# Two heads' half-array products pinned side by side, the first branch's keys and values formed once, negated scores, and one step moved from VectorE to ScalarE

## The chip, the cores and the metric

One core of one Trainium2 chip runs the whole program as a single launch. The metric is the device time of one execution in microseconds (us).

## The reference, cut to what matters

Two transformer blocks of 512 tokens by 1024 features, run one after the other, all in fp32. The first block has two attention branches with 8 heads of 64 features each. The first branch selects keys with an indexer and attends to a 128-wide latent `c_kv`; the second is a stick-breaking attention.

```python
# first branch (dsa)
q_abs = einsum("bshd,hcd->bshc", q, w_uk)
rel   = relu(einsum("bqhe,bse->bqhs", q_idx, k_idx))          # indexer, 8 heads of 64
score = einsum("bqhs,bqh->bqs", rel, w_idx)                   # causal, then top_k(score, 128)
logits = einsum("bqhc,bqkc->bhqk", q_abs, c_sel) * 0.125 + rel_bias[bucket(distance)]
o = einsum("bqhc,hcd->bqhd", einsum("bhqk,bqkc->bqhc", softmax(logits), c_sel), w_uv)
# second branch (stick breaking)
z = einsum("bqhd,bshd->bhqs", q, k) * 0.125
a = exp(log_sigmoid(z) + reversed_exclusive_cumsum(log_sigmoid(-z)))   # strictly causal
o = einsum("bhqs,bshd->bqhd", a, v)
# second block, its first layer: latent attention, 8 heads, 64 + 32 rotary features
o = einsum("bhqk,bkhd->bqhd", softmax(mask(einsum("bqhd,bkhd->bhqk", q, k) * 96**-0.5)), v)
```

Around this lie the input projections, gates, output products, a mixture of 32 experts, a recurrence, a retention layer and two MLPs, which the change doesn't touch.

## The kernel before, in words

Everything is fp32. A projection of weights is three passes of split operands (high by high, high by low, low by high; `mm3`, lines 128 to 130), the attention products are plain fp32 and appear in the trace as two records each. Lines 106 and 107 split a tile into its high and low part (ScalarE, then VectorE).

The program is unrolled and hands its instructions to a scheduler that fixes each engine's order ahead of time: earlier program text goes first, later work fills in where the scheduler expects an engine to be free and a buffer is to be had. Projections of later stages are what fills TensorE in the attention loops. An engine works through its own queue in order. Tiles of one tag share a fixed number of buffers; the first stage has 19 of tag "z" (projected queries, keys, values, masks and gates) and eight PSUM banks, two each of tags "a" (projections), "l" (scores), "x" (transposes) and "o" (value sums).

The pieces that the change and the prediction touch, by line of the kernel before:

- The indexer (lines 234 to 256): for each of the query blocks i = 1, 2, 3 and each pair of heads, two score products with 64 rows each (line 242), one head on rows 0 to 63 of the array and the other on rows 64 to 127, each into a bank of its own, for W = (i+1) x 128 keys. ScalarE applies relu (245), VectorE adds up (249) and then finds the top 128 in 16 rounds (253, 254).
- The second branch (lines 300 to 327), for each head pair `hp` and query block `i`: two score products (306), the mask as a bf16 product (308), tanh on ScalarE (310), a memset and a scaling step on VectorE (311, 312), the scan (313) and a product (315), transposes on TensorE (318), a copy out of PSUM on ScalarE (320), and the value products (326), which put one head on columns 0 to 63 and the other on 64 to 127 of one bank; then a split (109, 110).
- The first branch (lines 332 to 382), for each half of the heads `hg` and query block: the query goes through `w_uk` (343) and out of PSUM (344); each head's scores are a product of all 128 rows with the latent (349), get the bias (352, 354), the selection mask and maximum (357), a sign flip of the maximum (361), exp (363) and the division (364, 365), then transposes (368), a copy (370) and the product with the latent (372). Four heads later one copy (374) and the product with `w_uv` (379), then the split.
- The latent attention in the second block (`softmax`, lines 1121 to 1135, and `attend`, lines 1137 to 1162): maximum, sign flip (1129), exp (1131), transposes (1152), copy (1154), value products by column halves (1160). Its stage has three banks "l", one "x" and one "o". Its scores have 96 rows (1147).

In all these loops the two products of a pair are two separate entries for the scheduler, and it may put other work between them.

## Time and profile before

| | us |
|---|---|
| median of 3 runs | 2307.77 (2306.92 to 2308.5) |
| profiled execution | 2308.01 |
| its span in the trace | 2305.8 |
| TensorE busy | 2215.8 |
| VectorE busy | 1241.2 |
| ScalarE busy | 895.7 |

The profile is one execution. Busy is the time in which at least one instruction of an engine runs; a product on TensorE counts until its last result is out, so successive products overlap by the tail, and how long one holds the queue is read from where the next one starts. The granted clock (PEclk) is TensorE's, as a share of 2.4 GHz. A view of waits lists who sat idle until whom. In the timeline, successive instructions of one line and engine are merged into a row: start, duration, engine, line, output and inputs, rows by columns of the array and columns streamed, and the number of records.

### The profile page before, as it was taken

How to read it: one execution, taken by the hardware profiler on the slowest of the kernel's cores; microseconds unless marked ns; L12 is line 12 of the kernel's file. 1: busy time of each engine (PE TensorE's matmuls, PEld its weight loads, DVE VectorE, ACT ScalarE, POOL GpSimd, SP SyncE). 2: the span in 40 equal slices, each digit the busy share in tenths (PEclk: the TensorE clock that was granted, in tenths of full speed). 3: DMA queues.
4: the chain of work that ended last, by engine and by line, in shares of the span. 5: the costliest groups of instructions: out<-in, count | busy, mean ns of one | idle time of the engine just before them, and what ended most of it. 6: DMA issues, size and time to landing. Idle time of an engine off the chain costs nothing.

```text
span 2305.8 us, 35750 instructions
## 1 busy us (share of the span) xinstructions
PE 2215.8 (96%) x14228; PEld 1836.5 (80%) x14228; DVE 1241.2 (54%) x2423; ACT 895.7 (39%) x1710; POOL 194.6 (8%) x247
## 2 busy tenths in 40 slices
PE   7999999969999999998999999999999998999998
PEld 5766778954444697778999999888888888989888
DVE  5976554633333677667544435745454547343436
ACT  5234542422122565665422324532323235332334
POOL 0000000111111001005000001501010104000000
PEclk9989999979999999999999999999999999999999
DMA  6211113759999541014323334232222122233233
GB/s 215 74 56 37 46 46 96 247 210 390 396 399 401 194 143 57 24 42 151 99 87 91 91 92 128 89 97 78 84 69 92 66 82 93 82 101 92 86 103 122
DMA packets 107465, 296.71 MB, mean 129 GB/s; under 512 B 17286, under 2 KB 19345, under 8 KB 107297
## 3 DMA queue, kind: packets, MB, share of 16 engines
q1 hardware_dynamic: 102656, 285.81, 36.9%
q0 software_dynamic: 3488, 6.50, 0.8%
q8 instruction: 113, 1.85, 0.3%
q10 hardware_dynamic: 1152, 2.10, 0.2%
q14 instruction: 56, 0.45, 0.1%
HBM read 292.31 MB, written 6.37 MB: 130 GB/s over the span
## 4 chain that ended last, share of the span: by engine, by line
PE 68%; DVE 4%; POOL 2%; ACT 2%; issue 1%; DMA 1%; POOLq 0%; DVEq 0%; ACTq 0%; SPq 0%
PE ps L128 18%; PE ps L129 17%; PE ps L130 17%; PE ps L725 5%; PE ps L762 3%; PE ps L749 2%; DVE wl L107 1%; POOL t L919 1%; PE ps L1147 1%; PE ps L1160 1%; PE ps L713 1%; DVE X L107 1%; ACT wh L106 1%; DVE N L882 0%; PE ps L1152 0%
## 5 line engine op out<-in xcount | busy, mean ns | idle before, releaser
L128 PE MATMUL ps<-X,wh 128*128 128x512 f32 (+3 forms) x1728 | 571.1, 332 | 16.8 <-ACT wh L106 10.4
L106 ACT ACTIVATE wh<-wr 128x1024 fp32r<-128x1024 f32 (+1 forms) x325 | 336.2, 1038 | 622.8 <-PE ps L129 431.3
L129 PE MATMUL ps<-X,wh 128*128 128x512 f32 (+3 forms) x1728 | 569.8, 330 | 3.8 <-DVE X L107 3.5
L130 PE MATMUL ps<-X,wl 128*128 128x512 f32 (+3 forms) x1728 | 568.1, 330 | 0.2 <-DVE wl L107 0.2
L107 DVE TENSOR_TENSOR wl<-wr,wh 128x1024 fp32r<-128x1024 f32 (+1 forms) x325 | 394.0, 1214 | 237.2 <-ACT wh L106 235.4
L128 PEld LDWEIGHTS ps<-X,wh 128*128 128x128 f32 x1728 | 325.7, 189 | 49.8 <-ACT wh L106 10.4
L129 PEld LDWEIGHTS ps<-X,wh 128*128 128x128 f32 x1728 | 326.9, 189 | 35.7 <-DVE X L107 7.0
L130 PEld LDWEIGHTS ps<-X,wl 128*128 128x128 f32 x1728 | 326.0, 189 | 31.3 <-issue 2.7
L130 PE MATMUL ps<-h,wl 128*128 128x256 f32 (+1 forms) x512 | 146.7, 287 | 0.7 <-DVE wl L107 0.7
L128 PE MATMUL ps<-h,wh 128*128 128x256 f32 (+1 forms) x512 | 146.3, 286 | 0.7 <-ACT wh L106 0.7
L129 PE MATMUL ps<-h,wh 128*128 128x256 f32 (+1 forms) x512 | 146.7, 287 | 0.0
L129 PE MATMUL ps<-wl,h 128*128 128x256 f32 x512 | 144.4, 282 | 0.7 <-DVE wl L107 0.7
L128 PE MATMUL ps<-wh,h 128*128 128x256 f32 x512 | 144.0, 282 | 0.4 <-ACT R L1471 0.3
L130 PE MATMUL ps<-wh,h 128*128 128x256 f32 x512 | 143.5, 281 | 0.0
L129 PE MATMUL ps<-wl,X 128*128 128x256 f32 x448 | 127.5, 285 | 0.5 <-DVE wl L107 0.5
L128 PE MATMUL ps<-wh,X 128*128 128x256 f32 x448 | 128.0, 286 | 0.0
L130 PE MATMUL ps<-wh,X 128*128 128x256 f32 x448 | 127.1, 284 | 0.0
L130 PEld LDWEIGHTS ps<-h,wl 128*128 128x128 f32 x512 | 97.3, 190 | 0.9 <-DVE wl L107 0.9
L128 PEld LDWEIGHTS ps<-h,wh 128*128 128x128 f32 x512 | 97.0, 190 | 1.1 <-ACT wh L106 1.1
L128 PEld LDWEIGHTS ps<-wh,h 128*128 128x128 f32 x512 | 96.6, 189 | 0.9 <-ACT R L1471 0.6
L129 PEld LDWEIGHTS ps<-h,wh 128*128 128x128 f32 x512 | 97.0, 189 | 0.0
L129 PEld LDWEIGHTS ps<-wl,h 128*128 128x128 f32 x512 | 96.1, 188 | 1.0 <-DVE wl L107 0.9
(467 smaller groups left out, 3846.4 us busy)
## 6 DMA issues: line engine op xcount, KB each, us to landing
wr<-in_mlp_w_dram SPq DMA_DIRECT2D x104, 512.0 KB
X<-in_w_gu_dram SPq DMA_DIRECT2D x116, 256.0 KB
wr<-in_w_gu_dram SPq DMA_DIRECT2D x56, 512.0 KB
wr<-in_mlp_w2t_dram SPq DMA_DIRECT2D x40, 512.0 KB
wr<-in_w_in_dram SPq DMA_DIRECT2D x34, 512.0 KB
HF<-in_w_dn_dram SPq DMA_DIRECT2D x64, 256.0 KB
wr<-in_w_dn_dram SPq DMA_DIRECT2D x32, 512.0 KB
wr<-in_od_qkg_dram SPq DMA_DIRECT2D x32, 512.0 KB
```

What stands on the lines that cost most here:

```text
L106: SC.activation(hi, src, AF.Copy)
L107: V.tensor_tensor(lo, src, f(hi), op=OP.subtract)
L128: PE.matmul(dst, a[0], b[0], start=start, stop=False)
L129: PE.matmul(dst, a[0], b[1], start=False, stop=False)
L130: PE.matmul(dst, a[1], b[0], start=False, stop=stop)
L713: PE.transpose(pt[:, j, :], gs[pr][:, tt(4 * u + j)], ident)
L725: PE.matmul(pa[e * 64:e * 64 + 64, :], xT[:, k, e * 64:e * 64 + 64], wgs[8 * pr + k // 2 * 2 + e][k % 2], start=k == 0, stop=k == 7)
L749: PE.matmul(pa[e * 64:e * 64 + 64, :], hd[:, q * P + e * 64:q * P + e * 64 + 64], wds[4 * pr + 2 * q + e][u], start=q == 0, stop=q == 1)
L762: PE.matmul(pt, sts[pr - 1 + q][:, tt(s)], ys[pr - 1 + q][u][v][:, :S], start=q + v == 0, stop=q + v == 2)
L919: G.tensor_tensor(t[:, :w], t[:, :w], sh[:, :w], op=OP.add)
L1147: PE.matmul(pz[:, :W], qh[h][0:96, KEYS[i]], kh[h][0:96, :W], start=True, stop=False)
L1160: PE.matmul(po[v * 64:v * 64 + 64, :], vh[j][:, h * 64:h * 64 + 64], ats[v][:, tt(j)], start=j == 0, stop=j == i)
```

## The change

- `two_banks` allocates one PSUM tile of two banks; the score tiles of a head pair are its halves. Banks of the first stage become two such tiles "l" (four banks), two "a", one "x" and one "o".
- `row_pair` issues the two 64-row score products of a head pair, the second pinned behind the first on TensorE. It is used in the indexer, in the second branch and in the first branch.
- `column_pair` issues all value products of a head pair and query block as one pinned sequence, alternating between the two heads, that starts with the head that is ready last. It is used in the second branch, the first branch and `attend`.
- The first branch forms keys (`ka`, 4 tiles) and values (`va`, 4 tiles) from the latent once, by eight 512-column products, in place of taking each query through `w_uk` and each sum through `w_uv`. Scores then have 64 rows per head, and the loop runs over head pairs.
- Scores of the first branch and of the latent attention are negated, so that the minimum is at once the bias of the exponential and the sign flips go away. In the latent attention the scale moves into the keys.
- In the second branch the scaling step becomes a ScalarE copy with scale and bias, and the memset goes to GpSimd.
- Tag "z" has 21 buffers for 19, tag "q" goes away.

```diff
+    def two_banks():
+        t = bank((P, 2, 512), "l")
+        return t[:, 0, :], t[:, 1, :]
+
+    def behind(ins):
+        return tc.keep_in_program_order(ins)
+
+    def row_pair(outs, lhs, rhs, w, stop=True):
+
+        PE.matmul(outs[0][:, :w], lhs[0:64], rhs[0:64, :w], start=True, stop=stop)
+        with tc.high_priority():
+            behind(PE.matmul(outs[1][:, :w], lhs[64:128], rhs[64:128, :w], start=True, stop=stop))
+
+    def column_pair(po, values, ats, hp, n):
+
+        def one(j, v):
+            h = 2 * hp + v
+            return PE.matmul(po[v * 64:v * 64 + 64, :], values[j][:, h * 64:h * 64 + 64], ats[v][:, tt(j)],
+                             start=j == 0, stop=j == n - 1)
+
+        one(0, 1)
+        with tc.high_priority():
+            for j, v in [(j, v) for j in range(n) for v in (1, 0)][1:]:
+                behind(one(j, v))
+
...
-    Z, local, close1 = phase(dict(z=19, r=6, q=2, t=3, s=3, e=2, c=3), dict(a=2, l=2, x=2, o=2))
+    Z, local, close1 = phase(dict(z=21, r=6, t=3, s=3, e=2, c=3), dict(a=2, l=2, x=1, o=1))
...
-                pts = [bank(tag="l") for v in range(2)]
-                for v in range(2):
-                    r = slice(v * 64, v * 64 + 64)
-                    PE.matmul(pts[v][:, :W], qidx[h // 2][r, tt(i)], kidx[r, :W], start=True, stop=True)
+                pts = two_banks()
+                row_pair(pts, qidx[h // 2][:, tt(i)], kidx, W)
...
-        V.tensor_scalar(acc, acc, -2e38, NEG, op0=OP.is_gt, op1=OP.mult)
+        V.tensor_scalar(acc, acc, -2e38, -NEG, op0=OP.is_gt, op1=OP.mult)
...
-            at, pzs = [], [bank(tag="l") for v in range(2)]
-            for v in range(2):
-                r = slice(v * 64, v * 64 + 64)
-                PE.matmul(pzs[v][:, :W], qb[hp][r, tt(i)], kb[hp][r, :W], start=True, stop=False)
+            at, pzs = [], two_banks()
+            row_pair(pzs, qb[hp][:, tt(i)], kb[hp], W, stop=False)
             for pz in pzs:
                 PE.matmul(pz[:, W - P:W], identb, goneb, start=False, stop=True)
                 t, be = Z("s"), Z("e")
                 SC.activation(t[:, :W], pz[:, :W], AF.Tanh, scale=1.0 / 16)
-                V.memset(be[:, W:W + 1], 1.0)
-                V.tensor_scalar(be[:, :W], t[:, :W], -0.5, 0.5, op0=OP.mult, op1=OP.add)
+                G.memset(be[:, W:W + 1], 1.0)
+                SC.activation(be[:, :W], t[:, :W], AF.Copy, scale=-0.5, bias=0.5)
...
             po = bank((P, P), tag="o")
-            for j in range(i + 1):
-                for v in range(2):
-                    h = 2 * hp + v
-                    PE.matmul(po[v * 64:v * 64 + 64, :], vb[j][:, h * 64:h * 64 + 64], at[v][:, tt(j)],
-                              start=j == 0, stop=j == i)
+            column_pair(po, vb, at, hp, i + 1)
             split(po, ob[hp][0][:, tt(i)], ob[hp][1][:, tt(i)], scale=0.5)
 
-    qa = [proj(14 + c, Z("z")) for c in range(4)]
+
+    qa, ka, va = [proj(14 + c, Z("z")) for c in range(4)], [], []
+    for c in range(4):
+        pt = bank(tag="ox"[c % 2])
+        PE.matmul(pt, wuk[:, tt(c)], cT, start=True, stop=True)
+        ka.append(Z("z"))
+        SC.activation(ka[c][:, :S], pt, AF.Copy)
+    for s in range(4):
+        pt = bank(tag="ox"[s % 2])
+        PE.matmul(pt, cT[:, tt(s)], wuv, start=True, stop=True)
+        va.append(Z("z"))
+        SC.activation(va[s][:, :S], pt, AF.Copy)
     oa = [(big("HF", F32R), big("HF", F32R)) for hp in range(4)]
-    for hg in range(2):
+    for hp in range(4):
         for i in range(4):
             W = (i + 1) * P
             far = max(W - 256, 0)
             near = W - far
-            qab = Z("q")
-            qv = qab[:, :S].rearrange("p (a v b) -> p a v b", a=2, v=2)
-            for v in range(2):
-                pq = bank((P, 2, P), tag="o")
-                r = slice(v * 64, v * 64 + 64)
-                for u in range(2):
-                    PE.matmul(pq[:, u, :], wuk[r, 2 * hg + u, :], qa[2 * hg + u][r, tt(i)], start=True, stop=True)
-                SC.activation(qv[:, :, v, :], pq, AF.Copy, scale=0.125)
-            po = bank((P, 4, P), tag="o")
-            for hh in range(4):
-                h = hg * 4 + hh
-                pl = bank(tag="l")
-                PE.matmul(pl[:, :W], qab[:, tt(hh)], cT[:, :W], start=True, stop=True)
+            at, pls = [], two_banks()
+            row_pair(pls, qa[hp][:, tt(i)], ka[hp], W)
+            for v, pl in enumerate(pls):
+                h = 2 * hp + v
                 lg = Z("s")
                 if far:
-                    SC.activation(lg[:, :far], pl[:, :far], AF.Identity, bias=b31[:, h:h + 1])
-                o = (h % 2) * 256
-                V.tensor_tensor(lg[:, far:W], pl[:, far:W], rbias[h // 2][:, o:o + near][:, ::-1], op=OP.add)
+                    SC.activation(lg[:, :far], pl[:, :far], AF.Identity, scale=-0.125, bias=b31[:, h:h + 1])
+                V.scalar_tensor_tensor(lg[:, far:W], pl[:, far:W], -0.125, rbias[hp][:, v * 256:v * 256 + near][:, ::-1],
+                                       op0=OP.mult, op1=OP.subtract)
+
                 mx = tiny((P, 1), tag="mx", bufs=6)
                 if i:
-                    V.tensor_tensor_reduce(lg[:, :W], lg[:, :W], tmask[i], op0=OP.add, op1=OP.max, scale=1.0,
-                                           scalar=GONE, accum_out=mx)
+                    V.tensor_tensor_reduce(lg[:, :W], lg[:, :W], tmask[i], op0=OP.add, op1=OP.min, scale=1.0,
+                                           scalar=-GONE, accum_out=mx)
                 else:
-                    V.tensor_reduce(mx, lg[:, :W], axis=AX.X, op=OP.max)
-                V.tensor_scalar(mx, mx, -1.0, None, op0=OP.mult)
+                    V.tensor_reduce(mx, lg[:, :W], axis=AX.X, op=OP.min)
                 sm = tiny((P, 1), tag="sm", bufs=6)
-                SC.activation(lg[:, :W], lg[:, :W], AF.Exp, bias=mx, accum_out=sm)
+                SC.activation(lg[:, :W], lg[:, :W], AF.Exp, bias=mx, scale=-1.0, accum_out=sm)
                 V.reciprocal(sm, sm)
                 V.tensor_scalar(lg[:, :W], lg[:, :W], sm, None, op0=OP.mult)
-                pt = bank((P, 4, P), tag="x")
+                pt = bank((P, 4, P), "x")
                 for j in range(i + 1):
                     PE.transpose(pt[:, j, :], lg[:, tt(j)], ident)
                 pT = Z("c")
                 SC.activation(pT[:, :W], pt.rearrange("p a b -> p (a b)")[:, :W], AF.Copy)
-                for j in range(i + 1):
-                    PE.matmul(po[:, hh, :], ctok[:, j, :], pT[:, tt(j)], start=j == 0, stop=j == i)
-            oT = Z("e")
-            SC.activation(oT[:, :S], po.rearrange("p a b -> p (a b)"), AF.Copy)
-            pu = bank((P, 2, P), tag="o")
-            for hh in range(4):
-                h = hg * 4 + hh
-                r = slice((h % 2) * 64, (h % 2) * 64 + 64)
-                PE.matmul(pu[r, hh // 2, :], wuv[:, h, :], oT[:, tt(hh)], start=True, stop=True)
-            for u in range(2):
-                o = oa[hg * 2 + u]
-                split(pu[:, u, :], o[0][:, tt(i)], o[1][:, tt(i)])
+                at.append(pT)
+            po = bank((P, P), tag="o")
+            column_pair(po, va, at, hp, i + 1)
+            split(po, oa[hp][0][:, tt(i)], oa[hp][1][:, tt(i)])
...
+    scale = -(96 ** -0.5)
...
-                SC.activation(kh[2 * hp][0:64, hs], pt[0:64, :], AF.Copy)
-                V.tensor_copy(kh[2 * hp + 1][0:64, hs], pt[64:128, :])
+                SC.activation(kh[2 * hp][0:64, hs], pt[0:64, :], AF.Copy, scale=scale)
+                V.tensor_scalar(kh[2 * hp + 1][0:64, hs], pt[64:128, :], scale, None, op0=OP.mult)
             linear(fin, wkv, [kn], HALF2, nk=1, wo=hp * P, tag="l")
             for h in (2 * hp, 2 * hp + 1):
-                V.tensor_copy(kh[h][64:96, :], kpe[64:96, :])
+                V.tensor_scalar(kh[h][64:96, :], kpe[64:96, :], scale, None, op0=OP.mult)
...
         mx, sm = (tiny((P, 2), tag=t, bufs=6) for t in ("mx", "sm"))
-        nx = tiny((P, 1), tag="nx", bufs=6)
         for c, pz in enumerate(pzs):
-            V.tensor_reduce(mx[:, c:c + 1], pz[:, :w], axis=AX.X, op=OP.max)
+            V.tensor_reduce(mx[:, c:c + 1], pz[:, :w], axis=AX.X, op=OP.min)
         if n > 1:
-            V.tensor_tensor(mx[:, 0:1], mx[:, 0:1], mx[:, 1:2], op=OP.max)
-        V.tensor_scalar(nx, mx[:, 0:1], -scale, None, op0=OP.mult)
+            V.tensor_tensor(mx[:, 0:1], mx[:, 0:1], mx[:, 1:2], op=OP.min)
         for c, pz in enumerate(pzs):
-            SC.activation(p[:, c * w:(c + 1) * w], pz[:, :w], AF.Exp, bias=nx, scale=scale, accum_out=sm[:, c:c + 1])
+            SC.activation(p[:, c * w:(c + 1) * w], pz[:, :w], AF.Exp, bias=mx[:, 0:1], scale=-1.0, accum_out=sm[:, c:c + 1])
...
             po = bank((P, P), "o")
-            for j in range(i + 1):
-                for v in range(2):
-                    h = 2 * hp + v
-                    PE.matmul(po[v * 64:v * 64 + 64, :], vh[j][:, h * 64:h * 64 + 64], ats[v][:, tt(j)],
-                              start=j == 0, stop=j == i)
+            column_pair(po, vh, ats, hp, i + 1)
```

## Rows read from the trace of the kernel before

**Rows 1.** The page, busy time of each engine over the whole span.
```profile
PE 2215.8 (96%) x14228; PEld 1836.5 (80%) x14228; DVE 1241.2 (54%) x2423; ACT 895.7 (39%) x1710; POOL 194.6 (8%) x247
```

**Rows 2.** Table of stretches: us; busy (records) per engine; granted clock, DMA share, GB/s.
```profile
45.00:130.00 85.00, 83.68 (x435) 65.28 (x435) 81.41 (x187) 26.88 (x44) 0.00 (x0) 1.00 0.24 74
130.00:135.00 5.00, 3.20 (x18) 1.37 (x16) 4.86 (x10) 2.11 (x5) 0.00 (x0) 1.00 0.00 0
135.00:152.00 17.00, 15.75 (x40) 7.29 (x40) 8.93 (x29) 3.95 (x11) 1.02 (x1) 0.50 0.39 125
152.00:210.00 58.00, 57.45 (x341) 34.39 (x341) 46.77 (x120) 26.57 (x68) 0.00 (x0) 1.00 0.04 12
218.00:335.00 117.00, 117.00 (x654) 85.83 (x653) 65.47 (x220) 66.39 (x170) 0.00 (x0) 1.00 0.13 42
885.00:1030.00 145.00, 136.61 (x984) 105.64 (x983) 99.34 (x243) 93.97 (x226) 7.00 (x8) 0.96 0.11 34
```

**Rows 3.** Who TensorE waited for, 130 to 215 us: total, times, longest.
```profile
PE ps L318 <- DVE s L315: 3.5, 3, 3.1
```

**Rows 4.** Groups by line, 135 to 210: busy us, mean ns | idle before, releaser.
```profile
L320 ACT ACTIVATE c<-ps 128x128 f32<-128x128 f32 (+3 forms) x32 | 13.9, 438 | 25.6 <-PE ps L318 19.2 <-PE ps L308 6.0
L310 ACT ACTIVATE s<-ps 128x384 f32<-128x384 f32 (+3 forms) x29 | 12.7, 448 | 1.8 <-PE ps L308 1.5 <-DVE e L311 0.2
...
L312 DVE TENSOR_SCALAR e<-s 128x128 f32<-128x128 f32 (+3 forms) x32 | 10.0, 317 | 7.6 <-ACT s L310 7.6
```

**Rows 5.** Timeline of TensorE, 182 to 194: score products of one head alone.
```profile
182.58 1.12 PE L306 MATMUL ps<-z,z 64*128 64x512 f32 x2
183.63 0.55 PE L318 MATMUL ps<-c,s 128*128 128x128 f32 x3
...
185.50 0.49 PE L306 MATMUL ps<-z,z 64*128 64x128 f32 x2
...
187.73 0.70 PE L306 MATMUL ps<-z,z 64*128 64x256 f32 x2
...
193.99 0.91 PE L306 MATMUL ps<-z,z 64*128 64x384 f32 x2
```

**Rows 6.** Timeline of TensorE at 198: both heads' score products side by side.
```profile
198.64 1.13 PE L306 MATMUL ps<-z,z 64*128 64x512 f32 x4
```

**Rows 7.** Timeline of TensorE, 136 to 149: score products at half clock.
```profile
136.66 1.65 PE L306 MATMUL ps<-z,z 64*128 64x384 f32 x2
...
146.83 2.07 PE L306 MATMUL ps<-z,z 64*128 64x512 f32 x2
```

**Rows 8.** Timeline of TensorE, 915 to 918: value products of the latent attention.
```profile
915.10 0.43 PE L1160 MATMUL ps<-c,v 128*64 128x128 f32 x2
...
916.40 1.09 PE L1160 MATMUL ps<-c,v 128*64 128x128 f32 x14
```

**Rows 9.** Timeline of TensorE, 313 to 333: products of the first branch.
```profile
313.98 0.71 PE L343 MATMUL ps<-z,r 64*128 64x128 f32 x4
...
316.16 1.98 PE L349 MATMUL ps<-N,q 128*128 128x512 f32 x4
...
323.40 2.05 PE L372 MATMUL ps<-c,l 128*128 128x128 f32 x16
325.29 0.60 PE L368 MATMUL ps<-c,s 128*128 128x128 f32 x4
...
331.72 0.66 PE L379 MATMUL ps<-e,r 128*64 128x128 f32 x8
```

**Rows 10.** Who TensorE waited for, 880 to 1030: total, times, longest.
```profile
PE ps L1147 <- ACT p L1131: 2.6, 5, 1.1
PE ps L1160 <- ACT c L1154: 2.3, 4, 1.4
PE ps L1152 <- ACT c L1154: 1.5, 3, 0.7
```

**Rows 11.** One line's instructions: ns minimum/median/maximum, first and last start.
```profile
L1129 DVE TENSOR_SCALAR t<-t x34: 130/146/155, 893.8 to 1021.9; 128x1 f32<-128x1 f32 x34
```

More of the change, by code (lines that the diff above doesn't have):

```diff
@@ L179, in block_kernel @@
     rstd(rx, ssx, D, EPS1, 4)
-    pb = bank(tag="l")
+    pb = two_banks()[0]
     for s in range(4):
@@ L283, in block_kernel @@
     b31 = load(local((P, 8)), None, A["rel_bias"][31, :].partition_broadcast(P))
+    V.tensor_scalar(b31, b31, -1.0, None, op0=OP.mult)
     pt = bank()
@@ L288, in block_kernel @@
     SP.dma_start(bdist, negrow)
-    wuk = load(Z("r")[:, :S].rearrange("p (a b) -> p a b", b=P), "w_uk")
-    wuv = load(Z("r")[:, :S].rearrange("p (a b) -> p a b", b=64), "w_uv")
+    wuk = load(Z("r")[:, :S], "w_uk")
+    wuv = load(Z("r")[:, :S], "w_uv")
     rbias = [Z("r") for c in range(4)]
@@ L1115, in block_kernel @@
     negb, neg32b = local((P, P), BF16), local((P, 32), BF16)
-    V.tensor_copy(negb, negm)
-    V.tensor_copy(neg32b, neg32)
-    scale = 96 ** -0.5
+    V.tensor_scalar(negb, negm, -1.0, None, op0=OP.mult)
+    V.tensor_scalar(neg32b, neg32, -1.0, None, op0=OP.mult)
     att, rec = [], []
@@ L1537, in prep @@
     a["gone"] = np.where(c < r, 0.0, NEG).astype(np.float32)
-    wk = i["w_uk"][0].transpose(0, 2, 1)
     a["w_vb"] = chunks2(w[:, 2248:2760], 256)
-    a["w_uk"] = np.ascontiguousarray(wk.reshape(4, P, P).transpose(1, 0, 2))
-    a["w_uv"] = np.ascontiguousarray(i["w_uv"][0].transpose(1, 0, 2))
+    a["w_uk"] = np.ascontiguousarray(i["w_uk"][0].transpose(1, 0, 2).reshape(P, S))
+    a["w_uv"] = np.ascontiguousarray(i["w_uv"][0].transpose(1, 0, 2).reshape(P, S))
     a["rel_bias"] = i["rel_bias"]
```

## The prediction

> **What bounds the kernel now.** I read the page's busy line first. TensorE is busy 96% of the span, VectorE 54%, ScalarE 39% [rows 1]: a change is worth what it takes off TensorE's queue, as long as the two others can follow. Next the stretches the diff touches, in the table of stretches [rows 2]. 45 to 130 us is the indexer with its top-k: VectorE 81.4 of 85 us, TensorE 83.7. 135 to 210 is the second branch (stick breaking; "branch B" below): 135 to 152 at the granted clock 0.50 (the 1.2 GHz level), then 57.5 of 58 us busy at 1.00, VectorE 46.8. 218 to 335 is the first branch ("branch A"), TensorE 117.0 of 117 beside VectorE 65 and ScalarE 66. 885 to 1030 holds the latent attention, TensorE 136.6 of 145. A busy TensorE could still be waiting in its pipeline, so I read its waits: over 130 to 215 it waited only 3.5 us, nearly all in one wait at the start [rows 3]; for 215 to 335 the same view is empty. ScalarE's copies of transposed tiles, on the other hand, sat 25.6 us, mostly for TensorE [rows 4]. So in both branches TensorE's own queue sets the pace.
>
> **What a half-array product costs.** The fp32 products appear as two records (two passes). One 64-row score product alone, shown x2, lasts 0.49, 0.70, 0.91 and 1.12 us for 128, 256, 384 and 512 columns [rows 5]; the next starts 0.07 before that end (182.58 + 1.12 against 183.63), so it holds the queue 0.42, 0.63, 0.84 and 1.05 us, 2.94 for the four widths. Where both halves were queued side by side they show as x4 and last 1.13 us at 512 columns [rows 6]: two for the price of one. Of the 16 pairs of branch B in the timeline only three are side by side (one each at 128, 256 and 512 columns, the last of them in these rows); in the other 13 something stands between the halves. At half clock one product takes 1.65 (384) and 2.07 (512) [rows 7]. The value products use column halves: a lone one lasts 0.43, so holds 0.36; a run of 14 records (seven products) 1.09, holds 1.02 [rows 8]. A group of four key blocks is eight products; today it is that run plus one lone product, 1.38 in all, and with all in pairs it would be eight pass slots, as the run of 14 has (six shared, two single), so 1.02. The other sizes show the same pattern: each of the 16 groups loses one lone run of 0.36, and the paired groups cost 0.36, 0.58, 0.80, 1.02, together 2.76 per head pair.
>
> **The change, part by part.**
>
> Branch B, scores: 16 pairs at one price in place of two save 4 x 2.94 = 11.8, less the three already paired (0.42 + 0.63 + 1.05 = 2.1): 9.7; the two pairs at half clock save 0.74 and 0.95 more: 11.4. Values: 30 runs in the timeline become 16, 14 x 0.36 = 5.0, and twice that price for two of them in the half-clock stretch, 0.7 more (an estimate from the same doubling): 5.7. Together 17.1 us off TensorE. Does another engine become the bound? VectorE gives up the scaling step, 10.0 us [rows 4]; ScalarE gets 32 copies of the same shapes as its tanh, at 0.45 each 14.3. Over 135 to 210 that leaves VectorE 55.7 - 10.0 = 46, ScalarE 30.5 + 14.3 = 45 and TensorE 73 - 17 = 56 [rows 2]: TensorE remains the fullest, with far less margin. The one-column memset that goes to GpSimd adds a semaphore there, and the only step that reads that column comes after the scan, which hides it; I cost it at nothing, and at 32 x 0.146 = 4.7 us, the price of another one-column step [rows 11], if that cover is gone.
>
> Branch A: removed are the query-side product with w_uk (64 records, four in 0.71: 64/4 x 0.64 = 10.2), the 128-row scores (a 512-column one: four records 1.98, so 0.96 each; over the widths about 2.5 x 8 = 20), the value products against the latent (160 records, 16 in 1.89: 18.9) and the product with w_uv (eight in 0.66: 8 x 0.58 = 4.6) [rows 9]: 53.7 us. Added are eight 512-column products for keys and values, 8 x 0.96 = 7.7, the paired scores 11.8 and the paired values 4 x 2.76 = 11.0: 30.5. Net 23.2 off TensorE. VectorE loses 32 sign flips, ScalarE trades 24 copies for 8: neither was near 117 us. The eight new tiles take "z" buffers, of which there are 21 for 27 wanted, so the last of them wait for branch B's queries and keys; the first value product needs all it sums over. That cost lies between nothing and the eight products themselves (7.7); I take 1.5, since one head pair's buffers come free a quarter of the way through branch B.
>
> Both branches: the pairs take two two-bank tiles, so the transposes ("x") and the value sums ("o") have one bank each. TensorE must wait for the copy of one head before it transposes the next, and all it has queued stands behind that wait. The latent attention already works with one "x" and one "o" bank: there TensorE waited 1.5 us for those copies before transposes and 2.3 before value products, over 34 heads [rows 10]. I charge 3.8 per branch. The bounds are nothing and one copy, 0.44, for each of 32 heads, 14.0. The Trainium skill's page "TensorEngine Tiling (Array Packing)" (Restrictions and Gotchas, Gotcha 1) says row tiles must write different PSUM banks and so raise PSUM pressure. This kernel does pay it, with these two banks; no run so far shows the price.
>
> Latent attention: the same column grouping, 16 lone runs x 0.36 = 5.8; the scores have 96 rows and stay. 34 sign flips of 0.146 us leave the path from the maximum to the exponential [rows 11]; TensorE waited 2.6 us for that exponential [rows 10], of which I take 1.0. Scaling the keys instead of copying them costs what the copy did. Together 6.8.
>
> Indexer: 12 pairs at their best cost 4 x (0.63 + 0.84 + 1.05) = 10.1, and so much is saved at most, where no pair overlaps today. But VectorE, 96% busy with the top-k, ends that stretch [rows 2], and branch B waits for it. Between 0 and 10.1; I take 1, next to the end that the busy engine speaks for.
>
> Sum: branch B 17.1 - 3.8 = 13.3; branch A 23.2 - 1.5 - 3.8 = 17.9; latent attention 6.8; indexer 1: **39 us**. The profiled execution took 2308.0 us (2305.8 span and 2.2 around), the median is 2307.8. 2308.0 - 39 = **2269 us**. What follows (experts, later layers) starts earlier by the same.
>
> **Rivals.**
>
> 1. Everything comes through: no hand-off stalls, branch B's half-clock stretch ends too (some 4 us more), the indexer's gain is used. 17.1 + 4 + 23.2 + 6.8 + 4 = 55: 2253 us. For it: TensorE never waited inside the branches. Against: the single banks.
>
> 2. The hand-offs cost one copy (0.44 us) for every head of both branches. Branch B saves 17.1 - 14.0 = 3, branch A 21.7 - 14.0 = 8, the rest 8: 19, so 2289 us. For it: one bank, TensorE's queue in order, ScalarE with 14 us more work. Against: the latent attention's 3.8. The Trainium skill, same page (Performance Considerations, PSUM Bottleneck), states that tiling speeds TensorE but not the reading of PSUM, so that the copies may become the limit. The trace of before speaks against it, as ScalarE waited for TensorE; by that rule the outcome is this rival.
>
> 3. Slower. Place: the transposes behind the single "x" bank. If each copy also stands behind another head's ScalarE step, TensorE loses 0.44 + 0.45 = 0.89 us per head, 57 us over 64 heads, against the 47 that all parts save before hand-offs (17.1 + 21.7 + 6.8 + 1): 2318 us. It decides from 47/64 = 0.73 us per head. For it: filler projections, which covered 14 us of branch B, are few. Against: it needs sixfold the wait that the latent attention shows.
>
> 4. The change doesn't do what it says: pinned halves run one after the other. Then branch A still saves 53.7 - (7.7 + 23.5 + 16.8) = 6, the hand-offs take 8, and the sign flips give 1: about 2308, no change. Against: the x4 records of 1.13 us [rows 6].
>
> **How the numbers follow.** Chances: forecast 0.50 (its own range 2255 to 2282), everything 0.18, hand-offs 0.20, slower 0.08, nothing 0.04. The range 2244 to 2296 takes in the first, the second and most of the third, and the ends of the unknown costs. A change of this kernel can be told from none at about 0.2%, 4.6 us. Faster 0.87, same 0.05, slower 0.08.
>
> **What would show it.** Right: score pairs of all three loops as x4 records with starts within some ns of each other and 1.1 us at 512 columns; 16 runs of value products per loop; the branch B stretch near 62 us, branch A near 99; in the waits of TensorE, transposes waiting for ScalarE copies at 2 to 6 us per branch. Wrong: more than 15 us of such waits per branch (rival 2 or 3); x2 records of 1.1 us in sequence (rival 4); VectorE or ScalarE above 95% in branch B; or a granted clock of 0.50 over more than the 17 us of before, since a stretch with TensorE waiting more than it did at 130 to 135 (3.2 of 5 us busy) came just ahead of that fall [rows 2].

## The result, and the profile after

The changed kernel takes 2256.38 us (median of four, 2255.51 to 2258.7) beside 2307.35 for the kernel before: a ratio of 0.978 (95% interval 0.9763 to 0.9797), 51 us less. Run again later beside other kernels it took 2256.97 (2256.28 to 2257.49). The profiled execution took 2256.59, its span is 2254.8. The time lies inside the range and 12.6 us below the forecast; the first rival (everything comes through, 2253) is nearer to it than the forecast (2269).

The page's busy line of the changed kernel, beside [rows 1]: TensorE gave up 59 us of busy time, and its share stays at 96%.

```profile
PE 2156.5 (96%) x14116; PEld 1794.6 (80%) x14116; DVE 1226.2 (54%) x2294; ACT 900.0 (40%) x1726; POOL 197.9 (9%) x279
```

Where the 51 us went is read from three marks: the last addition that joins the two branches (L407 before, L419 after), the first score product of the latent attention (L1147, L1157) and its last transposition (L1152, L1162). The view of one line's instructions gives its first and last start: the last start is the mark for the addition and the transposition, the first start for the score product. First the kernel before, then the one after:

```profile
L407 DVE TENSOR_TENSOR z<-z,R x8: 683/687/692, 399.0 to 418.8; 128x512 f32<-128x512 f32 x8
L1147 PE MATMUL ps<-k,R x64: 272/484/1223, 889.8 to 1009.8; 96*128 96x128 f32 x16, 96*128 96x256 f32 x16, 96*128 96x384 f32 x16, 96*128 96x512 f32 x16
L1152 PE MATMUL ps<-c,p x80: 270/273/421, 902.1 to 1022.0; 128*128 128x128 f32 x80
```
```profile
L419 DVE TENSOR_TENSOR z<-z,R x8: 684/684/693, 358.1 to 378.0; 128x512 f32<-128x512 f32 x8
L1157 PE MATMUL ps<-k,R x64: 272/484/1222, 848.6 to 964.3; 96*128 96x128 f32 x16, 96*128 96x256 f32 x16, 96*128 96x384 f32 x16, 96*128 96x512 f32 x16
L1162 PE MATMUL ps<-c,p x80: 270/273/476, 860.1 to 975.9; 128*128 128x128 f32 x80
```

At the first mark the changed kernel is ahead by 418.8 - 378.0 = 40.8 us, at the second by 889.8 - 848.6 = 41.2, at the third by 1022.0 - 975.9 = 46.1, at the end by 2305.8 - 2254.8 = 51.0. So some 41 us come from the two branches, 5 from the latent attention, and 5 fall after it, in code that the change doesn't touch.

The pairs, in TensorE's timeline of the changed kernel from 180 to 200 us. Each half now has a line of its own (L100, L102), and the halves start within 10 ns of each other; a pair of 512-column products, two records each, holds the queue from 180.20 to 181.26, 1.06 us, which is what one lone product cost [rows 5]. A group of four key blocks is one run of 16 records:

```profile
180.20 0.69 PE L100 MATMUL ps<-z,z 64*128 64x512 f32 x1
180.21 0.69 PE L102 MATMUL ps<-z,z 64*128 64x512 f32 x1
180.73 0.59 PE L100 MATMUL ps<-z,z 64*128 64x512 f32 x1
180.74 0.59 PE L102 MATMUL ps<-z,z 64*128 64x512 f32 x1
181.26 0.44 PE L108 MATMUL ps<-c,z 128*64 128x128 f32 x4
...
191.40 1.09 PE L108 MATMUL ps<-c,z 128*64 128x128 f32 x16
```

The table of stretches, columns as in [rows 2]. 130 to 195 holds branch B, 195 to 205 the new keys and values, 205 to 268 branch A:

```profile
130.00:135.00 5.00, 2.99 (x18) 1.37 (x17) 4.90 (x11) 2.15 (x6) 0.00 (x0) 1.00 0.08 7
135.00:142.00 7.00, 5.52 (x20) 2.89 (x20) 5.82 (x12) 3.24 (x10) 0.49 (x5) 0.51 0.79 223
142.00:190.00 48.00, 47.48 (x350) 30.02 (x349) 40.92 (x72) 38.63 (x98) 3.40 (x26) 1.00 0.11 34
190.00:205.00 15.00, 15.00 (x65) 8.76 (x64) 4.04 (x5) 7.01 (x11) 0.00 (x0) 1.00 0.25 71
205.00:268.00 63.00, 61.09 (x410) 38.44 (x410) 51.08 (x175) 46.46 (x138) 0.69 (x2) 1.00 0.09 27
```

TensorE is 99% busy from 142 to 190 and 97% from 205 to 268, with VectorE at 85% and 81%: it still sets the pace, with less margin than before. The stretch at the granted clock 0.50 (the 1.2 GHz level) at 135 us is 6.8 us long instead of 17.1. And the two views of TensorE's waits, 130 to 195 and 195 to 270:

```profile
PE ps L340 <- DVE s L337: 3.5, 1, 3.5
PE ps L108 <- ACT c L342: 0.3, 1, 0.3
PE ps L340 <- ACT s L332: 0.2, 1, 0.2
```
```profile
PE ps L388 <- ACT c L390: 0.7, 3, 0.4
PE ps L388 <- DVE t L384: 0.6, 1, 0.6
PE ps L100 <- DVE s L373: 0.2, 1, 0.2
```

The 3.5 us are the wait of before [rows 3]. Waits for ScalarE's copies, which were to cost 3.8 us in each branch, are 0.3 and 0.7.

The time from 130 us to the first mark can be split in three. Each record of a product is charged from the end of the record before it (or from its own start, where that is later) to its own end; of what falls into a stretch at 0.50, half counts as work and half as added by the half clock; the rest is idle time of TensorE. The ends of records are modelled, so tenths are not to be trusted. In us:

| 130 us to the joined branches | length | products at the full clock | added by half clock | TensorE idle |
|---|---|---|---|---|
| before | 288.8 | 277.3 | 7.9 | 3.6 |
| after | 248.0 | 239.4 | 2.7 | 5.9 |
| e1, nothing pinned | 275.4 | 264.5 | 6.8 | 4.1 |
| e2, pins alone | 274.5 | 263.7 | 1.7 | 9.1 |
| e3, step on VectorE | 254.2 | 240.5 | 2.8 | 10.9 |
| e7, no fillers | 275.1 | 239.9 | 14.0 | 21.2 |
| e11, two queries first | 242.3 | 239.7 | 0.0 | 2.6 |

(e1 to e11 are the experiments below.) So the 40.8 us are 37.9 of products, 5.2 of half clock that is gone, less 2.3 of idle time that is new. By line, half clock included: half-array products and all products of the old branch A took 96.4 us before (L306 24.5, L326 17.4, and L343, L349, L372, L379 together 54.5); after it row pairs take 24.2, value products 22.7 and the new keys and values 7.2, together 54.1. Projections went from 161.4 to 159.5, masks and transposes from 26.7 to 28.3. The gross gain forecast for the branches was 17.1 + 23.2 = 40.3, of which 0.74 + 0.95 + 0.7 = 2.4 was half clock: 37.9 of products, which arrived whole. The half clock gave twice what the forecast had taken for it.

### The profile page after: what moved, and what is told of

It reads as the page before. It is cut to its first block, busy times and chain, and to the rows that moved or that the text cites. A ratio compares the mean times of both kernels' runs of the same rounds, so it can differ in the third digit from the quotient of the medians.

```text
span 2254.8 us, 35511 instructions
## 1 busy us (share of the span) xinstructions
PE 2156.5 (96%) x14116; PEld 1794.6 (80%) x14116; DVE 1226.2 (54%) x2294; ACT 900.0 (40%) x1726; POOL 197.9 (9%) x279
## 3 DMA queue, kind: packets, MB, share of 16 engines
q1 hardware_dynamic: 102656, 285.81, 37.9%
## 4 chain that ended last, share of the span: by engine, by line
PE 80%; DVE 9%; ACT 3%; issue 3%; POOL 2%; DMA 1%; POOLq 0%; SPq 0%; DVEq 0%; ACTq 0%
PE ps L153 21%; PE ps L155 21%; PE ps L154 21%; PE ps L737 5%; PE ps L774 3%; PE ps L761 2%; DVE wl L132 2%; PE ps L108 1%; DVE z L277 1%; DVE t L276 1%; ACT wh L131 1%; DVE X L132 1%; PE ps L725 1%; PE ps L1157 1%; PE ps L100 1%
## 5 line engine op out<-in xcount | busy, mean ns | idle before, releaser
L153 PE MATMUL ps<-X,wh 128*128 128x512 f32 (+3 forms) x1728 | 568.4, 330 | 16.9 <-ACT wh L131 10.2
L153 PEld LDWEIGHTS ps<-X,wh 128*128 128x128 f32 x1728 | 325.8, 189 | 47.3 <-ACT wh L131 10.1
L154 PE MATMUL ps<-wl,X 128*128 128x256 f32 x448 | 127.3, 284 | 0.5 <-DVE wl L132 0.5
```

Of the source, the lines that this page charges most:

```text
L153: PE.matmul(dst, a[0], b[0], start=start, stop=False)
L154: PE.matmul(dst, a[0], b[1], start=False, stop=False)
```

## The experiments

My theory after this result: the gain is TensorE's queue time, and the hand-offs that I charged are hidden by the projections that stand between the heads. The rivals: the gain is in something else (the steps taken from VectorE, the sign flips, the half clock), or the hand-offs are cheap in themselves. Marks of the profiled execution of every kernel, in us, as read above:

| kernel | branches joined | latent scores start | last latent transposition | span |
|---|---|---|---|---|
| before | 418.8 | 889.8 | 1022.0 | 2305.8 |
| after | 378.0 | 848.6 | 975.9 | 2254.8 |
| e1, nothing pinned | 405.4 | 867.4 | 997.0 | 2277.3 |
| e2, pins alone | 404.5 | 878.3 | 1010.5 | 2291.8 |
| e3, step on VectorE | 384.2 | 853.5 | 980.7 | 2260.9 |
| e4, other banks | 381.2 | 849.6 | 976.8 | 2255.8 |
| e5, latent products apart | 378.0 | 848.9 | 980.2 | 2260.6 |
| e6, flips back | 377.5 | 847.8 | 980.0 | 2258.9 |
| e7, no fillers | 405.1 | 876.3 | 1002.6 | 2282.4 |
| e8, no fillers, other banks | 415.1 | 883.0 | 1010.3 | 2290.4 |
| e9, four queries first | 381.1 | 851.2 | 977.6 | 2257.5 |
| e10, one query first | 371.5 | 841.6 | 968.9 | 2248.2 |
| e11, two queries first | 372.3 | 841.8 | 969.0 | 2248.1 |
| e12, changed kernel again | 378.7 | 849.9 | 977.0 | 2255.7 |

### Everything but the pins, and the pins alone

In e1 the helpers stay and the order is left to the scheduler again:

```diff
-        PE.matmul(outs[0][:, :w], lhs[0:64], rhs[0:64, :w], start=True, stop=stop)
-        with tc.high_priority():
-            behind(PE.matmul(outs[1][:, :w], lhs[64:128], rhs[64:128, :w], start=True, stop=stop))
+        for v in range(2):
+            r = slice(v * 64, v * 64 + 64)
+            PE.matmul(outs[v][:, :w], lhs[r], rhs[r, :w], start=True, stop=stop)
```

The value products are written as two plain loops, likewise without pins.

> The changed kernel with all its tiles, keys and values formed once and negated scores, but the products of a pair are again separate entries in the old order, without pins. Theory (the gain is queue time of TensorE, and the pins bring the pairs side by side): score pairs fall apart in the second and the first branch, one lone run of value products of 0.36 us per group comes back in both and in the latent attention; 17 us back in the second branch, up to 17.6 in the first, 5.8 in the latent attention, so 2285 to 2297 us. Rival (the keys and values formed once, the shorter VectorE path and the other banks carry the gain, and halves meet by themselves often enough): within 10 us of the changed kernel, 2256 to 2266.

Measured: 2283.75 us (2279.04 to 2292.31), ratio 0.9911 (0.989 to 0.9932). The timeline of e1 shows why: mask, transposes and value products stand between the halves, and each half pays alone.

```profile
154.39 0.91 PE L101 MATMUL ps<-z,z 64*128 64x384 f32 x2
155.23 1.09 PE L107 MATMUL ps<-c,z 128*64 128x128 f32 x14
156.25 0.33 PE L334 MATMUL ps<-c,s 128*128 128x128 f32 x1
156.41 0.22 PE L324 MATMUL ps<-l,c 128*128 128x128 bf16 x1
156.56 0.91 PE L101 MATMUL ps<-z,z 64*128 64x384 f32 x2
```

Of 44 row pairs 17 are parted (the indexer's stay together), and the value products of the three loops are 96 runs, where the changed kernel has 48. That nothing stands between the halves is not enough by itself: in the kernel before, 15 of its 28 pairs (11 of these 15 in the indexer) have nothing between, and in 11 of these the second half starts 0.13 to 0.54 us after the first. In e1 all 27 such pairs start within 10 ns. What e1 shares with the changed kernel there is the common tile of two banks, where the kernel before takes each half's bank by itself; no run tests that alone. Of the 27.4 us by which the branches end later (405.4 - 378.0), 25.1 are products and 4.1 half clock, less 1.8 of idle time. By the end the loss is 22.5 in the profiled execution, above all since a half-clock stretch of 20 us at the end of the first layer is missing in e1 (the last section). The time is 1 us below the theory's range and far from the rival's: side by side is worth some 25 us of products in the branches.

e2 is the kernel before with two-bank tiles, one bank each for transposes and value sums, and pinned pairs in the indexer, branch B and the latent attention, and nothing else of the change. Branch A keeps its old form, which has no such pairs.

> The kernel before with the two-bank score tiles, the pinned pairs in the indexer, the second branch and the latent attention, and one bank each for transposes and value sums; first branch, sign flips and the VectorE step as before. Theory: the second branch saves its 17 us and the latent attention 5.8, less hand-offs, so 2282 to 2290 us. Rival (the first branch's new form carries it): above 2300. Rival (single banks cost about a copy per head): above 2300 as well, but then with more than 15 us of waits of TensorE for the copies of transposes, where the first has few.

Measured: 2293.76 us (2288.88 to 2294.45), ratio 0.9936 (0.9919 to 0.9953), 14.0 us less than before by the spans, and 4 to 12 us above what was expected. The branches end 14.3 us earlier: 13.6 of products, 6.2 of half clock, less 5.5 of new idle time. The latent attention, whose value products are pinned too, takes 132.2 us as before: the trace has 17.0 us of half clock inside it, 912 to 922 and 997 to 1004, where the kernel before has 10.2 (more on this at e6). And in the branches VectorE is now late. The waits of TensorE in e2, 130 to 420:

```profile
PE ps L339 <- DVE s L336: 7.2, 10, 3.6
PE ps L108 <- DVE e L332: 1.6, 3, 0.7
```

By the spans e1 gained 28.5 us, e2 14.0, the whole change 51.0, which is 8.5 more than the two; by the mark of the branches, 13.4, 14.3 and 40.8, it is 13.1 more. Most of that is the pins of branch A, which are in neither of the two: in e1 branch A has 6 parted pairs and 33 runs of value products for 16, some 5 and 6 us at the prices of a lone product and a lone run (an estimate from [rows 5] and [rows 8]).

### The step on VectorE, and the banks

e3 puts the scaling step and the memset of branch B back on VectorE.

> The changed kernel with the scaling step and the one-column memset of the second branch back on VectorE, so that VectorE has 11.8 us more there and ScalarE 14 less. Theory (TensorE's queue sets that branch): 0 to 5 us slower, 2256 to 2261. Rival (VectorE had become what the branch waits for, and the moved step is a large part of the gain): 8 to 12 us slower, 2264 to 2268. A third way (ScalarE had become the bound): faster, below 2254.

Measured: 2261.87 us (2254.69 to 2264.55), ratio 0.9799 (0.978 to 0.9817): between what the two expected. The mark says more than the times: the branches end at 384.2, 6.2 us later, and TensorE's waits in branch B are those of e2 (130 to 270 us):

```profile
PE ps L340 <- DVE s L337: 7.5, 12, 3.5
PE ps L108 <- DVE e L333: 1.6, 3, 0.7
```

So the step on ScalarE is what lets VectorE keep up once the pairs are fast: 4.0 of the 6.2 us are a longer wait for the product after the scan, and 1.6 another wait for the same chain.

e4 shares the banks otherwise: `dict(a=2, l=1, x=2, o=2)`, one two-bank tile for scores, and two banks each for transposes and value sums.

> The changed kernel with the first stage's PSUM shared out otherwise: one two-bank score tile in place of two, two banks each for transposes and value sums. Theory (hand-offs at single banks cost TensorE next to nothing, since filler projections stand between): nothing gained by the second banks, and the single score tile makes the next pair wait for both heads' readers, 2256 to 2264 us. Rival (the forecast's charge of 3.8 us per branch or more is paid at the single banks): 4 to 8 us faster, 2248 to 2252.

Measured: 2261.13 us (2257.51 to 2263.84), ratio 0.9805 (0.979 to 0.982). The waits for copies are gone from its view of waits, and one for VectorE has grown (130 to 270 us):

```profile
PE ps L340 <- DVE s L337: 6.1, 11, 1.0
PE ps L388 <- DVE s L385: 0.6, 1, 0.6
```

With one score tile the next pair's scores start later, and VectorE with them. The branches end 3.2 us later, though the half clock at 135 us is missing here. The time lies in the theory's range and the rival falls: the single banks are no loss against this.

### The latent attention

e5 writes its value products in the loops of before, free to be parted.

> The changed kernel, but the value products of the latent attention are issued one by one again, free for the scheduler to part; everything else of the change stays. My theory: the side-by-side value products are what the latent attention gained (16 lone runs of 0.36 us = 5.8; the trace shows 5.2 less between the start of its scores and its end), so this kernel takes 4 to 6 us more than the changed one: 2260 to 2263 us, with some 30 runs of value products in that loop instead of 16. Rival: that gain came from the sign flips that are gone, or from how the half-clock stretches fell; then the time stays at 2255 to 2258 us though the runs of value products are more.

Measured: 2262.3 us (2261.45 to 2263.02), ratio 0.9802 (0.9786 to 0.9819), 5.9 over the changed kernel, as the theory had it. The trace is the changed kernel's up to the latent attention, which has 32 runs instead of 16 and lasts 980.2 - 848.9 = 131.3 us instead of 127.3. So 4.0 us are lost in the loop; 1.5 more come behind it, where the two kernels are the same but for the last value products, and stay open.

e6 puts a one-column VectorE step where the sign flips were (`V.tensor_scalar(mx, mx, 1.0, None, op0=OP.mult)`), 32 in branch A and 34 in the latent attention.

> The changed kernel with one more one-column VectorE step (times 1.0) on each head's extreme value, where the sign flip had stood, in the first branch (32) and in the softmax of the latent attention (34). My theory: TensorE's queue sets the pace, so the step costs nothing in the first branch and at most 1 us in the latent attention: 2255 to 2259 us. Rival: the steps stand on the path from the scores to the exponential and cost their own length, 66 x 0.146 = 9.6 us, or 4.8 if only one of the two loops is so: 2261 to 2266 us.

Measured: 2263.0 us (2260.67 to 2263.85), ratio 0.9807 (0.9791 to 0.9823). That lies in the rival's range, and my theory missed. The marks split it: branch A, with 32 steps of 0.146 us, ends at 377.5, no later than without; the latent attention takes 980.0 - 847.8 = 132.2 us, 4.9 more. Much of that lies beside a half-clock stretch at 881 us that the changed kernel doesn't have, in all 17.0 us of half clock in that loop against 10.2. The same stretch in e6 and in the changed kernel:

```profile
881.00:892.00 11.00, 10.15 (x24) 5.72 (x24) 6.37 (x22) 5.68 (x17) 0.00 (x0) 0.53 0.02 6
```
```profile
881.00:892.00 11.00, 10.11 (x62) 7.64 (x61) 7.25 (x20) 7.17 (x19) 0.00 (x0) 1.00 0.04 12
```

At the same busy time 24 records instead of 62. The split of above, taken from the first latent score to the last transposition, sets the four combinations of pins and flips side by side (us):

| latent attention | length | products at the full clock | added by half clock | TensorE idle |
|---|---|---|---|---|
| before: flips, no pins | 132.2 | 120.2 | 4.8 | 7.2 |
| e2: flips, pins | 132.2 | 114.1 | 8.3 | 9.8 |
| e5: no flips, no pins | 131.3 | 119.6 | 5.1 | 6.6 |
| e6: flips, pins | 132.2 | 114.0 | 8.4 | 9.8 |
| after: no flips, pins | 127.3 | 113.3 | 4.9 | 9.1 |

The pins take 6 us of products off in either case. What the flips cost beside the pins is 0.7 us of idle time (the wait for the exponential alone grows by 1.5, from 2.4 to 3.9, others shrink), 0.7 of products and 3.5 by the clock. The stretch at 881 us comes 34 us after the first latent score in e6 and again in e2 (912 us), the two kernels that have both pins and flips; the nine profiles with pins and without flips have 6.8 to 10.2 us of half clock in that loop, late in it. So the stretch goes with the flips, as far as these profiles tell; how they bring it about, no run shows.

### What hides the hand-offs

e7 pins the first product of each projection that the scheduler put inside branch A (the fillers) behind that branch.

> The changed kernel, but the first product of each group of projections that the scheduler put between the heads of the first branch is pinned behind that branch, so that no filler work stands there. My theory: the fillers are what covers the copies out of the single transpose bank and the single bank of value sums. Without them TensorE waits over 10 us inside the branch, much of it before transposes and value products for ScalarE's copies, the branch itself takes 50 to 60 us instead of 63, and the projections, some 27 us, come after it: 2268 to 2285 us. Rival: the copies are short beside the heads' other steps, TensorE's waits for copies stay under 3 us, and the time is lost only to VectorE's steps or not at all: TensorE's waits name VectorE, or the time stays under 2262 us.

Measured: 2287.45 us (2282.71 to 2292.26), ratio 0.9917 (0.9895 to 0.9938). The branches end 27.1 us later. Branch A has lost its fillers, and yet its transposes run from 208.5 to 266.8, 58.3 us, against 57.5 with fillers (207.9 to 265.4). The waits of TensorE in e7, 205 to 268, and its stretch 214 to 231:

```profile
PE ps L108 <- ACT c L394: 5.5, 10, 0.7
PE ps L392 <- DVE s L389: 3.5, 4, 1.2
PE ps L392 <- DVE HF L132: 2.9, 3, 1.2
PE ps L392 <- ACT c L394: 2.7, 6, 0.7
PE ps L100 <- DVE s L377: 1.2, 4, 0.4
PE ps L392 <- DVE s L377: 0.7, 1, 0.7
PE ps L392 <- DVE t L388: 0.6, 1, 0.6
```
```profile
214.00:231.00 17.00, 14.61 (x68) 8.25 (x68) 10.20 (x39) 9.43 (x30) 0.00 (x0) 0.51 0.01 2
```

17.1 us of waits instead of 1.5, of which 8.2 for copies and 8.9 for VectorE; and 27 us at half clock (17.1 from 214, 10.2 from 262), where the changed kernel has none from 205 to 268. Of the 27.1 us, 15.3 are idle time and 11.3 half clock by the split. So the hand-offs are not cheap in themselves, the fillers hide them, and they hide VectorE's chain as much as ScalarE's copies. The time is 2.5 us above what I had expected, since I hadn't counted the half clock.

e8 is e7 with the banks of e4. It tells a single bank from the data: a second bank can spare TensorE the wait for an earlier head's copy, not for the copy that it is about to read.

> The kernel without fillers in the first branch, and with the PSUM banks shared otherwise: one two-bank tile for scores instead of two, but two banks for transposes and two for value sums. If the copies from single banks are the price that shows when nothing covers them (my theory), this one is 4 to 12 us faster than the kernel without fillers and one score tile. Rival: the score tiles are the scarcer resource when nothing else is there to do (the next pair's scores cannot start before both heads have left the tile); then it is 3 us or more slower than that kernel.

Measured: 2294.03 us (2292.16 to 2295.91), ratio 0.9943 (0.9926 to 0.9959): 6.6 us slower than e7, so the rival holds, though for another place: branch B, whose scores have one tile as in e4, is where it loses. There TensorE waits 8.2 us for the product after the scan (130 to 205 us), where e7 waits 3.5, and 10.2 us of half clock follow at 200. In branch A (205 to 275 us) its largest waits are

```profile
PE ps L392 <- DVE s L389: 5.0, 6, 1.3
PE ps L108 <- ACT c L394: 4.6, 8, 0.6
PE ps L100 <- DVE s L377: 2.2, 5, 0.6
...
```

The 2.7 us of transposes waiting for copies are gone, but of the 5.5 us in which value products waited for copies 4.6 are still there: that is the wait for the data. So 2.7 us is about what a single transpose bank costs branch A bare, and under its fillers 0.7. The branch itself is no shorter for the second bank here: its transposes take 58.1 us (218.9 to 277.0) beside 58.3 in e7.

### Cover moved to where TensorE waits

What is left in the branches is the wait of 3.5 us at 130 us and the half clock behind it. e9 moves the four query projections of branch A in the text ahead of branch B's loop; e10 moves one of them, e11 two. The edit of e11:

```diff
+    qa = [proj(14 + c, Z("z")) for c in range(2)]
...
-    qa, ka, va = [proj(14 + c, Z("z")) for c in range(4)], [], []
+    qa += [proj(14 + c, Z("z")) for c in range(2, 4)]
+    ka, va = [], []
```

> The changed kernel with the first branch's four query projections moved in the text ahead of the second branch's loop, so that they can stand where TensorE waits 3.5 us for the first scan (130 to 135 us), just ahead of the half-clock stretch at 135 us (6.8 us long). My theory: the wait and the half clock behind it are what is left to be had there; with work in that gap both go or shrink, and the kernel takes 2250 to 2254 us, faster than the changed one. Rival: the projections already serve as cover later in the two branches; taken from there they leave TensorE waiting for copies and VectorE there, and the time is the same or longer, 2255 to 2263 us.

> The changed kernel with one of the first branch's four query projections ahead of the second branch's loop, the other three left behind it. With all four ahead, the wait of 3.5 us and the half clock at 135 us went, but the end of that branch ran out of cover: TensorE worked 4.3 of 7 us from 196 to 203 and a half-clock stretch of 10.2 us followed. One projection is some 5.5 us of work, enough for the gap of 3.5 us. My theory: the gap closes, the cover at the end stays, and the kernel takes 1 to 6 us less than the changed one run beside it. Rival: whichever cover is moved is missed elsewhere (or the half clock falls in another place), and the two are within 1 us, or this one is longer.

> As the one before, with two of the four projections ahead of the loop, some 11 us of work. My theory: the gap at 130 us is closed twice over and half of the cover at the end is gone, so the time lies between those of the kernels with one and with four moved: 0 to 4 us less than the changed kernel. Rival: as soon as the gap is closed any more cover moved is lost at the end, and it is longer than the changed kernel by 1 to 4 us.

> The changed kernel itself, beside the two others on the same chip, as their measure: 2255 to 2259 us. Every theory expects the same of it.

Measured: e9 2260.29 us (2258.49 to 2261.65), ratio 0.9797 (0.9784 to 0.981), the rival. e10 2252.52 (2244.0 to 2256.56), 0.9757 (0.9737 to 0.9777), and e11 2249.88 (2243.07 to 2254.56), 0.9744 (0.9723 to 0.9764), beside 2256.97 for the changed kernel (e12) on the same chip. Every run of e11 is below every run of e12, by 7.1 us at the median, more than I had expected of it; e10's is 4.5 less, as expected. In both profiles the branches end 5.7 to 6.5 us earlier than in the changed kernel. Stretches of e9, then of e11:

```profile
130.00:135.00 5.00, 5.00 (x23) 4.09 (x23) 4.90 (x10) 0.81 (x1) 0.00 (x0) 1.00 0.12 10
135.00:142.00 7.00, 7.00 (x32) 5.73 (x31) 3.25 (x4) 1.92 (x2) 0.00 (x0) 1.00 0.79 225
196.00:203.00 7.00, 4.28 (x30) 2.16 (x29) 5.99 (x12) 5.60 (x17) 0.40 (x4) 0.99 0.24 75
203.00:213.00 10.00, 7.99 (x41) 5.33 (x42) 4.72 (x7) 3.11 (x7) 0.95 (x1) 0.50 0.00 0
```
```profile
130.00:135.00 5.00, 5.00 (x22) 3.91 (x22) 4.90 (x10) 1.04 (x2) 0.00 (x0) 1.00 0.01 3
135.00:142.00 7.00, 7.00 (x34) 5.42 (x32) 3.26 (x4) 1.69 (x2) 0.00 (x0) 1.00 0.82 222
196.00:203.00 7.00, 7.00 (x38) 4.31 (x37) 2.02 (x3) 3.23 (x6) 0.00 (x0) 1.00 0.25 75
```

With work at 130 us the wait is gone and the clock stays at 1.00 there: by the split, e11's 5.7 us are 2.7 of half clock and 3.3 of idle time, less 0.3. With four projections moved the cover is short at the end of branch B instead, and the half clock comes there. With one or two it is enough in both places: e11 is the fastest kernel of this study.

## Why the prediction was right, and where it was not

- **What bounds the kernel: right.** TensorE's queue. What came off it in the branches, 40.8 us, came off the time.
- **Price of a pair and of a run: right.** 1.06 us for two 512-column products; 16 runs of value products per loop; 37.9 us of products came off the branches, as forecast. That pairs would show as x4 records was wrong, since the halves have a line each now. Two readings of before were off by little: of branch B's 13 pairs that are not side by side, 12 have something between the halves, and one (384 columns, at 177 us) has nothing between and starts its second half 0.54 us late; and in the indexer, where no pair was to overlap, one pair is side by side and ten overlap in part.
- **Hand-offs: the step that failed.** 3.8 us per branch were charged, from the latent attention's waits [rows 10]; 0.3 and 0.7 were measured. The rows were taken from a loop with waits of its own, where the question was what covers them here. The third rival called the filler projections few. They are not: e7 shows that branch A alone had some 15 us of waits hidden under them. Of the 1.5 for the wait of the new values nothing is there either: TensorE works through 190 to 205 without a gap. In all 7.6 + 1.5 = 9.1 us were charged, and TensorE's idle time rose by 2.3: 6.8 of the 12.0 us by which the span fell more than forecast.
- **Half clock: luck.** The forecast left the stretch at 135 us as it was and took 2.4 us from products inside it. It became 6.8 us long instead of 17.1, which gave 5.2: 2.8 more, where the first rival had some 4. Why it became shorter is open: the wait of 3.5 us ahead of it is still there.
- **The second rival** (one copy, 0.44 us, per head) fell for the same reason. The rule that stands beside it, in the Trainium skill's page "TensorEngine Tiling (Array Packing)" (Performance Considerations, PSUM Bottleneck), is stated for a fourfold speedup: the copies out of PSUM may then become the limit. Here two products go side by side, and the rule doesn't show: TensorE waited 1.0 us for copies. e7 has 8.2 us of such waits in one branch once the cover is gone.
- **The margin of VectorE: right in kind.** Without the step moved to ScalarE it would have been the next to be late: 6.2 us at the mark in e3.
- **Branch stretches:** branch B, first to last transposition, went from 70.5 us (136.3 to 206.8) to 53.8, where about 62 had been forecast for its window of 75. Branch A's 99 us were wrong: it takes 57.5, since projections that had stood in it now come after it. Its end says little, so the 40.8 is read behind both.
- **Indexer: 0 to 10.1, taken 1.** The last of the top-k steps starts at 132.1 instead of 132.5: 0.4. VectorE ends that stretch.
- **Latent attention: 6.8 forecast, 4.9 measured.** The 5.8 of the value products came off the queue (6.3 between e5 and the changed kernel), but TensorE idles 2.5 us more there, which the sum left at nothing: the waits that a shorter queue leaves bare are the term that it lacked. With 0.2 of half clock 4.0 are left, and the flips make the rest: 0.9 between before and e5.
- **After 976 us: 0 forecast, 4.9 measured.** One half-clock stretch of 3.4 us fewer is part of it (1893 and 1913 us before, one at 1869 after; 1.7 at most). The rest, by the split above products of code that is the same, stays open.

The parts add up: 40.8 - 32.2 = 8.6 from the branches and the indexer (6.8 of idle time, 2.8 of half clock, less the 1 taken for the indexer), 0.4 up to the latent attention, -1.9 from it, 4.9 behind it, together 12.0, which is the span's 51.0 less the 39 of the forecast.

## What to carry to other kernels

Ask of a new wait not how long it is in another loop but what work stands ready to cover it; take the cover away in one run and the waits show bare. Two half-array products cost one only where nothing stands between them in the queue and both may start at once. Left to the scheduler, 17 of 44 pairs fell apart, so here the order had to be pinned; and once they are cheap the engine that feeds them wants a look. Cover is worth most just ahead of a wait that one knows: moving two projections there gave 7 us, moving four took it back.

## What was not expected of the hardware

TensorE's granted clock moves the time of such a kernel by several us in either direction, in places that the change doesn't touch. Two profiles of the same code at the end of the first attention layer, the changed kernel and then e1, around the same wait of TensorE:

```profile
410.00:415.00 5.00, 3.06 (x28) 2.85 (x27) 4.29 (x9) 3.79 (x8) 1.68 (x3) 0.99 0.55 194
415.00:435.00 20.00, 20.00 (x98) 20.00 (x97) 5.04 (x10) 6.81 (x14) 1.68 (x3) 0.50 0.23 79
```
```profile
440.00:445.00 5.00, 3.65 (x30) 3.23 (x30) 4.02 (x8) 2.52 (x8) 1.68 (x3) 1.00 0.83 254
445.00:465.00 20.00, 19.57 (x154) 17.92 (x155) 6.93 (x11) 8.57 (x19) 0.54 (x1) 1.00 0.44 150
```

After a gap of the same 1.9 us in the same wait the one does 98 records in 20 us at 0.50, the other 154 at 1.00. With it e1 wins back 8.6 of the 27.4 us that it had lost (867.4 - 848.6 = 18.8 at the start of the latent scores). Over the whole span the half-clock stretches add up to 91 us before, 77 after, 63 in e1, 104 in e7 and 116 in e8. What makes one gap bring the lower level and another not, these runs don't settle; that with the gap at 130 us filled the clock stayed up from there to 142 us they show three times (e9, e10 and e11).
